# Probabilities times values in matmuls 256 columns wide, and the outputs of attention taken from PSUM by head pair

## The chip, the cores and the metric

The kernel runs on one core of a Trainium2 chip. Its time is the device time in microseconds, the median of three runs. The engines of the core are called PE (TensorE matmuls), PEld (its weight loads), DVE (VectorE), ACT (ScalarE), POOL (GpSimd) and SP (SyncE, which here only issues DMAs). Each engine works through its instructions in order; engines wait for each other by semaphores.

## The reference

One encoder layer over 512 tokens of width 1024, in float32. Two attentions run on one projection of the normalised input, their outputs are normalised, projected and added, and a mixture of experts follows.

```python
qa, ka, va, cq, ckv, kr = jnp.split(h @ w_in[l], IN_SPLITS, axis=-1)
out_a = windowed_gqa_sink(qa, ka, va, a_sink[l])     # A: 8 heads in 2 groups, |i-j| <= 128, a sink logit per head
out_b = mla_attention(q_nope, q_rope, k_nope, k_rope, v_b)   # B: 8 heads, all 512 keys
mixed = jnp.concatenate([rms_norm(out_a, out_norm_a_g[l]), rms_norm(out_b, out_norm_b_g[l])], axis=-1) @ w_out[l]
h = layer_norm(DEEPNORM_ALPHA * h + mixed, ln_attn_g[l], ln_attn_b[l])
ffn = hierarchical_moe(h, ...)    # top group of 4, top 2 of its 8 experts; 32 experts of 1024 -> 2 x 256 -> 1024
h = layer_norm(DEEPNORM_ALPHA * h + ffn, ln_ffn_g[l], ln_ffn_b[l])
```

Inside both attentions a head's output is `softmax(scores) @ v`, with 64 columns of v per head.

## The kernel before

Tokens are cut into four query tiles of 128 (t = 0 to 3). The stages are: layer norm and input projection (up to about 110 us), the two low-rank projections of B (to about 152), attention B (to about 240), attention A (to about 310), a hand-ordered tail that finishes tile 3, routes the tokens and gathers the first rows (to about 345), and the experts in 16 pairs with a closing layer norm. Up to the tail the order on each engine is set by a scheduler that lists instructions by priority and by a modelled time; in A the attention's own instructions are raised in priority by 200 (`tc.high_priority(200)`). The tail and the experts stand in an order written out by hand.

A unit of attention is one tile and one head. `attend` (L601) walks over 32 units, tile by tile and head by head. In step i it makes the scores of unit i, the transposes of unit i-2, and, every second step, the value matmuls of units i-4 and i-3. For B the scores are three matmuls of 512 columns into one of two PSUM banks (`scores_b`, L563, by `mm3`, L212); DVE takes the row maximum (L568), ACT the exponential with its row sum (L571), DVE the reciprocal (L557), and DVE or POOL, by the parity of the head, multiplies by it (L558). `probs_t` (L593) turns the 128x512 probabilities with four PE transposes (L596) and copies them to SBUF (L598), ACT and DVE in turn in B, ACT alone in A. The value matmuls (L619) hold 64 columns of v as weights and stream 128 columns of turned probabilities; head h0 of a pair goes to output partitions 0 to 63, head h1 to 64 to 127, each accumulated over the key tiles (4 in B, 2 or 3 in A). A tile's eight heads fill one PSUM bank (`pac`, of which there is one) in four 128-column parts.

When a tile is done, `finish` (L528) copies the bank to SBUF as a high part (`oh`, ACT) and a low part (`ol`, DVE), squares it (ACT), adds the squares of the four parts (DVE, L537), and projects: 2 x 4 triples of matmuls of 512 columns (L213 to L215 into `pwo`), one summing matmul (L547) for the norm, and an addition to the residual z (L552). `finish` is a generator: `tick` moves it on by a part after each unit, one generator at a time in B and two in A, so that projections fill PE between units. Tile 3 of A is finished in the tail (L1028 to L1085) instead.

The weights of an expert are gu (2 MB, gate and up) and dn (1 MB, down), in a ring of six slots in SBUF; the slots' space is lent to attention first (`tag=`). SP issues their loads in program order, and a load waits at the head of the queue until its space is free. In step 12 of A the kernel asks for pair 0 (slots 0 and 1, gu and dn), and gu of slots 3 and 4 (L1006 to L1008); after the tail for gu2 and dn2 (in the space of A's queries and keys), gu5, dn5, dn4, dn3 (L1226 to L1229), and then for each next pair as a slot comes free.

Of the kernel before, what the change touches and what calls it, by code (L numbers as in the profile page):

```python
# [26 lines left out]
H = 8  # L27
# [44 lines left out]
def build(tc, A, out):  # L72
# [24 lines left out]
    with top:  # L97
# [430 lines left out]
        def finish(t, po, wo):  # L528

            woh, wol = wo  # L530
            oh = fin.tile([P, 4, P], F32R, name="aoh", bufs=2)
            ol = fin.tile([P, 4, P], F32R, name="aol", bufs=2)
            split(po.rearrange("p (a b) -> p a b", a=4), oh, ol)
            sq = fin.tile([P, 4, P], F32, name="asq")
            SC.activation(sq.rearrange("p a b -> p (a b)"), po, AF.Square)
            s1 = fin.tile([P, P], F32, name="asum")
            V.tensor_reduce(s1, sq.rearrange("p a b -> p b a"), AX.X, ALU.add)  # L537
            yield
            for c in range(2):
# [14 lines left out]

        def normed(pr, den, n, eng):
# [7 lines left out]
        def scores_b(t, h):  # L563
# [8 lines left out]
            return normed(pr, den, S, V if h % 2 else PO)  # L572

        def scores_a(t, h):
# [16 lines left out]
            return normed(pr, den, nk, V)  # L591

        def probs_t(pr, n, ev):  # L593
# [3 lines left out]
            pT = scr.tile([P, S], F32, name="pT", bufs=3)  # L597
            ev(pT[:, :n * P], pt[:, :n * P])  # L598
            return pT

        def attend(units, done, hook, width, evs, boost=ExitStack):  # L601

            prs, pts = {}, {}
            n = len(units)
            for i in range(n + 3):
                with boost():
                    if i < n:
                        t, h, sfn = units[i][:3]
                        prs[i] = sfn(t, h)
                    if 2 <= i < n + 2:  # L610
                        pts[i - 2] = probs_t(prs.pop(i - 2), units[i - 2][5], evs[i % 2])
                    if i >= 4 and i % 2 == 0:
                        (t, h0, _, vfn, k0, nk), h1 = units[i - 4], units[i - 3][1]
                        if h0 == 0:
                            po = pac()
                        pp = pts.pop(i - 4), pts.pop(i - 3)
                        for k in range(nk):
                            for j, h in enumerate((h0, h1)):
                                PE.matmul(po[64 * j:64 * j + 64, h0 // 2 * P:h0 // 2 * P + P], vfn(k0 + k, h),  # L619
                                          pp[j][:, k * P:(k + 1) * P], start=(k == 0), stop=(k == nk - 1))  # L620
                        if h1 == H - 1:
                            done(t, po)
# [3 lines left out]
        wob = wout(woh, wol, 512, gob, lambda k: bp.tile([P, D], F32, name="wfo", bufs=2))  # L626
# [5 lines left out]
        attend([(t, h, scores_b, lambda k, h: vb[k][:, h, :], 0, NT) for t in range(NT) for h in range(H)],  # L632
               lambda t, po: side.append(finish(t, po, (woh, wol))), later, 1, (SC.copy, V.tensor_copy))
# [364 lines left out]
        units = []  # L998
        for t in range(NT):
            k0, k1 = max(0, t - 1), min(NT, t + 2)  # L1000
            units += [(t, h, scores_a, lambda k, h: va[:, k, 64 * (h // 4):64 * (h // 4) + 64], k0, k1 - k0)
                      for h in range(H)]
# [542 lines left out]
```

## Time and profile before

| | us |
|---|---|
| median of 3 runs | 599.52 (599.49 to 602.42) |
| profiled execution | 598.21 |
| its span, first to last instruction | 596.6 |
| PE busy in the span | 533.2 (89%) |
| DVE, ACT, POOL busy | 332.9, 204.5, 124.5 |
| moved by DMA | 141.8 MB, 238 GB/s on average |

The profile is of one execution. A busy PE is not a PE at its peak, since the printed duration of a matmul reaches to its modelled end and overlaps the next; what one costs in a stream is read from start to start. Times within the trace count from the span's start.

### The profile page before, as it was taken

To read this page: it belongs to the slowest core of one execution; us is meant where nothing else is said; L and a number is where in the kernel's file an instruction comes from. 1 tells how busy PE (TensorE), PEld (TensorE's weight loads), DVE (VectorE), ACT (ScalarE), POOL (GpSimd) and SP (SyncE) were. 2 spreads that over 40 slices of the span, in tenths; PEclk is the share of its full clock that TensorE was granted. 3 is DMA by queue.
4 is the path that set the end of the run, shared out by engine and by line. 5 is a ranking of instruction groups with operands and counts; after the bars stand their busy time and mean duration, and the time that the engine had idled before them with its cause. 6 is when DMAs were issued, how large, how long until landed. Compare 5 with 4: busy or idle time off the path is not lost. (4 is left out here: it accounts for less than half of the span.)

```text
span 596.6 us, 8402 instructions
## 1 busy us (share of the span) xinstructions
PE 533.2 (89%) x2946; PEld 343.5 (58%) x2947; DVE 332.9 (56%) x887; ACT 204.5 (34%) x429; POOL 124.5 (21%) x157
## 2 busy tenths in 40 slices
PE   2899999999899999999998989999998699879860
PEld 1688898799777777777777643443443233323230
DVE  5946473765777765988867744435334222102277
ACT  2266442454564453766441221211111111102132
POOL 2701121311433332213100121122211101100041
PEclk9999999999899999999998999999999989979985
DMA  8973400421211003992034899999999999999663
GB/s 286 299 256 77 132 11 1 129 81 41 88 37 37 1 1 107 331 421 105 36 142 182 306 345 414 418 414 417 417 413 397 421 419 405 406 424 415 261 271 141
DMA packets 46268, 141.77 MB, mean 238 GB/s; under 512 B 12379, under 2 KB 19419, under 8 KB 37008
## 3 DMA queue, kind: packets, MB, share of 16 engines
q1 hardware_dynamic: 40608, 131.06, 57.6%
q0 software_dynamic: 4464, 8.06, 3.6%
q10 hardware_dynamic: 1152, 2.10, 0.9%
q8 instruction: 24, 0.39, 0.3%
q14 instruction: 20, 0.16, 0.1%
HBM read 133.14 MB, written 16.25 MB: 250 GB/s over the span
## 5 line engine op out<-in xcount | busy, mean ns | idle before, releaser
L1184 PE MATMUL p_gu<-w_gu,xT 128*64 128x512 f32 x512 | 125.7, 614 | 15.2 <-DMA w_gu<-in_w_gu 14.3
L1184 PEld LDWEIGHTS p_gu<-w_gu,xT 128*64 128x64 f32 x512 | 40.7, 141 | 95.4 <-issue 68.0
L1189 DVE TENSOR_TENSOR hid<-hid,p_gu 128x256 f32<-128x256 f32 x16 | 6.7, 421 | 113.0 <-ACT hid L1188 113.0
L1188 ACT ACTIVATE hid<-p_gu 128x256 f32<-128x256 f32 x16 | 6.1, 384 | 176.8 <-PE p_gu L1184 165.0
L1204 PE MATMUL p_y<-w_dn,hidT 128*64 128x512 f32 x256 | 58.5, 598 | 1.0 <-issue 0.6
L1217 DVE SCALAR_TENSOR_TENSOR xg<-p_y,wsl,xg 128x512 f32<-128x512 f32 x30 | 23.5, 790 | 25.8 <-PE p_y L1204 25.3
L995 POOL DMA_INDIRECT xg<-norm_rows,tok x16 | 16.5, 1030 | 101.5 <-issue 23.7
L1210 POOL DMA_INDIRECT moe_rows<-xg,idx x15 | 15.6, 1038 | 98.9 <-DVE xg L1217 74.2
L596 PE MATMUL ptr<-cst,pr 128*128 128x128 f32 x208 | 35.3, 282 | 0.0
L1204 PEld LDWEIGHTS p_y<-w_dn,hidT 128*64 128x64 f32 x256 | 17.1, 136 | 30.3 <-issue 28.2
L558 POOL TENSOR_SCALAR pr<-pr,rc 128x512 f32<-128x512 f32 x16 | 25.0, 1564 | 44.1 <-DVE rc L557 44.1
L598 ACT COPY pT<-ptr 128x512 f32<-128x512 f32 (+2 forms) x48 | 22.6, 477 | 30.4 <-PE ptr L596 26.3
L596 PEld LDWEIGHTS ptr<-cst,pr 128*128 128x128 f32 x208 | 24.8, 143 | 7.7 <-issue 4.7
L571 ACT ACTIVATE pr<-pmm,bnm 128x512 f32<-128x512 f32 x32 | 22.0, 689 | 16.1 <-DVE bnm L568 13.5
L568 DVE TENSOR_REDUCE bnm<-pmm 128x1 f32<-128x512 f32 x32 | 21.8, 685 | 4.6 <-PE pmm L215 4.4
L215 PE MATMUL pmm<-wh,htl 128*128 128x512 f32 (+1 forms) x64 | 23.9, 374 | 0.0
L213 PE MATMUL pmm<-wh,hth 128*128 128x512 f32 (+1 forms) x64 | 23.8, 372 | 0.0
L619 PE MATMUL pac<-pT,vb 128*64 128x128 f32 x256 | 23.7, 282 | 0.0
L214 PE MATMUL pmm<-wl,hth 128*128 128x512 f32 (+1 forms) x64 | 23.5, 368 | 0.0
L590 ACT ACTIVATE pr<-sm,anm 128x257 f32<-128x257 f32 (+1 forms) x32 | 18.1, 567 | 10.2 <-PE ptr L596 5.9
L558 DVE TENSOR_SCALAR pr<-pr,rc 128x512 f32<-128x512 f32 (+2 forms) x48 | 20.9, 440 | 1.1 <-PE pmm L581 0.5
L215 PE MATMUL pwo<-wh,htl 128*128 128x512 f32 (+1 forms) x56 | 20.7, 370 | 0.0
(334 smaller groups left out, 1178.3 us busy)
## 6 DMA issues: line engine op xcount, KB each, us to landing
w_gu<-in_w_gu SPq DMA_DIRECT2D x52, 1024.0 KB, 16.6
w_dn<-in_w_dn SPq DMA_DIRECT2D x20, 1024.0 KB, 18.5
w_dn<-in_w_dn SPq DMA_DIRECT2D x24, 512.0 KB, 14.6
w_gu<-in_w_gu SPq DMA_DIRECT2D x24, 512.0 KB, 16.6
wf<-in_w_in SPq DMA_DIRECT2D x12, 512.0 KB, 6.5
moe_rows<-zr SPq DMA_DIRECT2D x8, 512.0 KB, 7.0
rows<-moe_rows SPq DMA_DIRECT2D x8, 512.0 KB, 8.8
wf<-in_w_q_b SPq DMA_DIRECT2D x12, 192.0 KB, 2.4
```

The lines of the kernel that those rows point to most:

```text
L213: PE.matmul(ps, ah, bh, start=first, stop=False)
L214: PE.matmul(ps, ah, bl, start=False, stop=False)
L215: PE.matmul(ps, al, bh, start=False, stop=last)
L558: eng.tensor_scalar(pr[:, :n], pr[:, :n], rc, None, ALU.mult)
L568: V.tensor_reduce(nm, sp, AX.X, ALU.max, negate=True)
L571: exps_.append(SC.activation(pr[:, :S], sp, AF.Exp, bias=nm, accum_out=den).ins)
L596: PE.transpose(pt[:, k * P:(k + 1) * P], pr[:, k * P:(k + 1) * P], ident)
L598: ev(pT[:, :n * P], pt[:, :n * P])
L619: PE.matmul(po[64 * j:64 * j + 64, h0 // 2 * P:h0 // 2 * P + P], vfn(k0 + k, h), pp[j][:, k * P:(k + 1) * P], start=(k == 0), stop=(k == n ...
L1184: PE.matmul(pg[64 * i:64 * i + 64], xT[:, j, 64 * i:64 * i + 64], ws[i][0][j], start=(j == 0), stop=(j == 7))
L1204: r = PE.matmul(py[64 * i:64 * i + 64, :], hT[:, j, 64 * i:64 * i + 64], ws[i][1][n][:, j], start=(j == 0), stop=(j == 1))
L1217: V.scalar_tensor_tensor(y, py, pl["wsl"], y, ALU.mult, ALU.add)
```

## The change

The value matmuls get 256 columns: in B a unit is still one tile and one head, but two tiles go together (`tp`), and for a pair of heads (`hp`) the four units' turned probabilities stand side by side by tile, so that one matmul streams both tiles of a head. In A two heads of a group, which have the same values, stand side by side; the two groups go to the two halves of the output partitions. That puts A's heads in another order on the partitions, and the rows of w_out and its gain are put in that order on the host.

In B, the bank `pac` is now filled per pair of heads and of tiles (128 x 256) and emptied each time: two casts and a square on ACT, two subtractions and an addition of squares on DVE (`out_b`). `finish` is left for A, its projection is `project` for both; the reduction of squares on DVE is gone, and A's squares are summed by four matmuls instead of one. The multiplication by the reciprocal goes from POOL and DVE to ACT and DVE, half and half (in A: from DVE alone). The space of dn0 serves to stage B's half of w_out and to hold the outputs of tiles 2 and 3, that of dn1 holds turned probabilities of A; so the loads of dn0 and dn1 leave the early group and follow dn2.

```diff
+        def project(t, oh, ol, sums, wo):
...
-                            PE.matmul(sp[:, 0:1], s1, iota1[:, 0:1], start=True, stop=True)
+                            for q, s1 in enumerate(sums):
+                                PE.matmul(sp[:, 0:1], s1, iota1[:, 0:1], start=(q == 0), stop=(q == len(sums) - 1))
...
-            eng.tensor_scalar(pr[:, :n], pr[:, :n], rc, None, ALU.mult)
+            if eng is SC:
+                SC.mul(pr[:, :n], pr[:, :n], rc)
+            else:
+                eng.tensor_scalar(pr[:, :n], pr[:, :n], rc, None, ALU.mult)
...
-            return normed(pr, den, S, V if h % 2 else PO)
+            return normed(pr, den, S, SC if t % 2 else V)
...
-            return normed(pr, den, nk, V)
+            return normed(pr, den, nk, SC if h // 4 else V)
...
+        def out_b(tp, hp, pT):
+            po = pac()
+            for k in range(NT):
+                for j in range(2):
+                    PE.matmul(po[64 * j:64 * j + 64, :2 * P], vb[k][:, 2 * hp + j, :],
+                              pT[j][:, k].rearrange("p a b -> p (a b)"), start=(k == 0), stop=(k == NT - 1))
...
+            for i in range(2):
+                split(pv[:, i], ohs[i][:, hp], ols[i][:, hp])
+            if hp == 0:
+                SC.activation(s1, pv, AF.Square)
+            else:
+                sq = tpb.tile([P, 2, P], F32, name="bsq", bufs=2)
+                SC.activation(sq, pv, AF.Square)
+                V.tensor_tensor(s1, s1, sq, ALU.add)
+            if hp == 3:
+                for i in range(2):
+                    side.append(project(2 * tp + i, [ohs[i][:, k] for k in range(4)], [ols[i][:, k] for k in range(4)],
+                                        [s1[:, i]], (woh, wol)))
...
+        def out_a(t, quad, pT, k0, nk):
...
+            for k in range(nk):
+                for g in range(2):
+                    PE.matmul(po[64 * g:64 * g + 64, 2 * P * quad:2 * P * quad + 2 * P], va[:, k0 + k, 64 * g:64 * g + 64],
+                              pT[g][:, k].rearrange("p a b -> p (a b)"), start=(k == 0), stop=(k == nk - 1))
...
-                h2["w0"] = load_pair(0, (0, 1))
+                h2["w0"] = [load_gus(i, i) for i in range(2)]
...
         gu2, dn2 = load_gus(2, 2), load_dn(2, 2)
+        h2["w0"] = [(gu, load_dn(i, i)) for i, gu in enumerate(h2["w0"])]
```

How it moves instructions is seen in the listing of each engine's program. On PE, at the first head pairs of B, before (L596 the transposes, L619 the value matmuls of a pair of heads, L213 to L215 the scores):

```order
L596 MATMUL ptr<-cst,pr 128x128 x4
L619 MATMUL pac<-pT,vb_1174 64x128
L213 MATMUL pmm<-kth,qth 128x512
L214 MATMUL pmm<-ktl,qth 128x512
L215 MATMUL pmm<-kth,qtl 128x512
L596 MATMUL ptr<-cst,pr 128x128 x4
L619 MATMUL pac<-pT,vb_1174 64x128
L619 MATMUL pac<-pT,vb_1175 64x128 x2
L619 MATMUL pac<-pT,vb_1176 64x128 x2
L619 MATMUL pac<-pT,vb_1177 64x128 x2
```

The same place now (L604 the transposes, L638 the value matmuls of two heads and two tiles):

```order
L604 MATMUL ptr<-cst,pr 128x128 x8
L213 MATMUL pmm<-kth,qth 128x512
L214 MATMUL pmm<-ktl,qth 128x512
L215 MATMUL pmm<-kth,qtl 128x512
L638 MATMUL pac<-pTb,vb_1174 64x256
L213 MATMUL pmm<-kth,qth 128x512
L214 MATMUL pmm<-ktl,qth 128x512
L215 MATMUL pmm<-kth,qtl 128x512
L604 MATMUL ptr<-cst,pr 128x128 x8
```

In both, a group of value matmuls is split: the first one stands alone and the other seven stand together further on. Such a group comes once per two units before and once per four now. Over all of B the listing of before has 31 uninterrupted runs of value matmuls, of 128 in all, and that of now 13, of 64.

On PE in the middle of A, tile 1, before (L580 and L581 the scores, L547 a tile's sum):

```order
L580 MATMUL pmm<-kall,q_85 128x384
L581 MATMUL pmm<-kall,q_85 128x384
L619 MATMUL pac<-pT,va 64x128 x2
L596 MATMUL ptr<-cst,pr 128x128
L619 MATMUL pac<-pT,va 64x128
L596 MATMUL ptr<-cst,pr 128x128
L619 MATMUL pac<-pT,va 64x128
L596 MATMUL ptr<-cst,pr 128x128
L619 MATMUL pac<-pT,va 64x128
L596 MATMUL ptr<-cst,pr 128x128 x3
```

A group of A now (L586 and L587 the scores, L1046 the value matmuls, `pTa` the turned probabilities of one group of heads):

```order
L1046 MATMUL pac<-pTa_2936,va 64x256
L586 MATMUL pmm<-kall,q_85 128x384
L587 MATMUL pmm<-kall,q_85 128x384
L1046 MATMUL pac<-pTa_2969,va 64x256
L1046 MATMUL pac<-pTa_2936,va 64x256
L1046 MATMUL pac<-pTa_2969,va 64x256
L1046 MATMUL pac<-pTa_2936,va 64x256
L1046 MATMUL pac<-pTa_2969,va 64x256
L604 MATMUL ptr<-cst,pr 128x128 x6
```

A's runs become fewer and longer: 32 with 80 matmuls before, 15 with 40 now.

On SP, the loads between the last of the early group and gu5 (`w_gu_3832` and `w_gu_3834` are gu2, `w_dn_3836` is dn2, `w_dn_3838` to `w_dn_3843` are dn0 and dn1, `w_gu_3846` is gu5), now:

```order
L692 DMA w_gu_2896<-in_w_gu 128x2048
L692 DMA w_gu_3832<-in_w_gu 128x2048
L692 DMA w_gu_3834<-in_w_gu 128x2048
L712 DMA w_dn_3836<-in_w_dn 128x2048
L709 DMA w_dn_3838<-in_w_dn 128x1024
L709 DMA w_dn_3839<-in_w_dn 128x1024
L709 DMA w_dn_3842<-in_w_dn 128x1024
L709 DMA w_dn_3843<-in_w_dn 128x1024
L692 DMA w_gu_3846<-in_w_gu 128x2048
```

Before, dn0 stood right behind the mask and dn1 among the early gu loads, and gu5 followed dn2 directly.

## Rows read from the trace of the kernel before

**Rows 1.** The page's slices: the span in 40 equal parts, the mean share of the DMA engines in tenths.

```profile
DMA  8973400421211003992034899999999999999663
```

**Rows 2.** Busy time by engine in a stretch of the experts' stage; the columns are the length in us, then for each engine its busy time and its instructions, then the clock granted to PE as a share of full speed, the mean DMA share and GB/s.

```profile
350.00:560.00 210.00, 190.06 (x902) 75.12 (x902) 67.00 (x178) 31.75 (x45) 29.60 (x28) 0.98 1.01 410
```

**Rows 3.** The same view in slices of 5 us around the end of attention A.

```profile
305.00:310.00 5.00, 5.00 (x45) 3.98 (x45) 2.87 (x17) 1.37 (x4) 0.55 (x1) 1.00 0.09 39
310.00:315.00 5.00, 4.64 (x31) 3.69 (x29) 2.52 (x6) 1.81 (x4) 0.55 (x1) 1.00 0.00 0
315.00:320.00 5.00, 5.00 (x29) 3.86 (x29) 3.53 (x12) 0.00 (x0) 0.00 (x0) 1.00 0.01 3
```

**Rows 4.** The timeline of SP's DMA issues there, gu2's second half and gu5: start, time, line, target and source, count; merged issues stand under their first.

```profile
298.68 0.33 SPq L653 DMA_DIRECT2D w_gu<-in_w_gu  x1
...
319.74 0.80 SPq L653 DMA_DIRECT2D w_gu<-in_w_gu  x2
```

**Rows 5.** Busy time by engine in the stretch of B, in that of A, and in one slice of 5 us of B (columns as in rows 2).

```profile
152.60:240.20 87.60, 85.46 (x586) 64.58 (x584) 62.99 (x142) 45.46 (x105) 29.52 (x28) 0.98 0.16 53
240.20:310.00 69.80, 68.68 (x454) 52.36 (x454) 58.68 (x196) 40.87 (x110) 14.64 (x38) 1.00 0.56 213
...
175.00:180.00 5.00, 4.62 (x31) 3.17 (x30) 4.55 (x11) 4.57 (x9) 1.56 (x1) 1.00 0.53 134
```

**Rows 6.** Groups of instructions of PE in both attentions: busy time and mean ns of one, then the engine's idle time before them and what ended it.

```profile
L619 PE MATMUL pac<-pT,va 128*64 128x128 f32 x160 | 18.7, 288 | 0.8 <-ACT pT L598 0.8
L213 PE MATMUL pmm<-kth,qth 96*128 96x512 f32 x32 | 15.3, 478 | 1.7 <-ACT pr L571 1.7
```

**Rows 7.** The timeline of PE in B, at the end of A's scores, and in the tail: start, time to the modelled end of the last of a merged row, line, target and sources, count.

```profile
166.08 0.43 PE L619 MATMUL pac<-pT,vb 128*64 128x128 f32 x2
166.44 0.50 PE L213 MATMUL pmm<-kth,qth 96*128 96x512 f32 x1
166.78 0.39 PE L214 MATMUL pmm<-ktl,qth 96*128 96x512 f32 x1
...
167.93 0.40 PE L214 MATMUL pmm<-ktl,qth 96*128 96x512 f32 x1
168.16 0.40 PE L215 MATMUL pmm<-kth,qtl 96*128 96x512 f32 x1
168.49 1.09 PE L619 MATMUL pac<-pT,vb 128*64 128x128 f32 x14
169.50 0.66 PE L596 MATMUL ptr<-cst,pr 128*128 128x128 f32 x4
170.09 0.43 PE L619 MATMUL pac<-pT,vb 128*64 128x128 f32 x2
...
173.21 0.66 PE L619 MATMUL pac<-pT,vb 128*64 128x128 f32 x8
173.80 1.10 PE L596 MATMUL ptr<-cst,pr 128*128 128x128 f32 x8
...
298.37 0.28 PE L581 MATMUL pmm<-kall,q 128*128 128x256 f32 x1
...
311.87 1.05 PE L1085 MATMUL psd<-cst,asq 128*128 128x1 f32 x8 [0.26 <-ACT asq L1076]
312.78 0.48 PE L1028 MATMUL pwo<-woah,aoh 128*128 128x512 f32 x1
```

**Rows 8.** The timeline of PE in the experts' stage: the down projection of a pair, eight matmuls of 512 columns that go to the two halves of the columns in turn, and what starts after it.

```profile
425.88 3.65 PE L1204 MATMUL p_y<-w_dn,hidT 128*64 128x512 f32 x16
429.36 4.03 PE L1184 MATMUL p_gu<-w_gu,xT 128*64 128x512 f32 x18
```

**Rows 9.** Groups of ACT and of POOL (columns as in rows 6): in B, in A, and, the last two, over the span.

```profile
L558 POOL TENSOR_SCALAR pr<-pr,rc 128x512 f32<-128x512 f32 x16 | 25.0, 1564 | 44.1 <-DVE rc L557 44.1
L571 ACT ACTIVATE pr<-pmm,bnm 128x512 f32<-128x512 f32 x32 | 22.0, 689 | 16.1 <-DVE bnm L568 13.5 <-DVE rc L557 1.4 <-PE ptr L596 1.1
L598 ACT COPY pT<-ptr 128x512 f32<-128x512 f32 x16 | 9.3, 584 | 18.9 <-PE ptr L596 18.8
L571 ACT ACTIVATION_READ_ACCUMULATOR pr<-pmm,bnm 128x1 f32 x32 | 6.3, 197 | 0.0
L535 ACT ACTIVATE asq<-pac 128x512 f32<-128x512 f32 x3 | 1.8, 594 | 0.5 <-DVE aol L209 0.5
...
L590 ACT ACTIVATE pr<-sm,anm 128x385 f32<-128x385 f32 x16 | 9.9, 619 | 7.9 <-PE ptr L596 5.9 <-issue 1.3 <-DVE rsq_t L181 0.4
L774 ACT ACTIVATE z<-z,ln_nb,ln_rs 128x512 f32<-128x512 f32 x2 | 1.5, 804 | 0.0
...
L420 ACT COPY va<-pmm 128x128 f32<-128x128 f32 x2 | 0.5, 272 | 0.4 <-DVE rp L329 0.4
L410 ACT ACTIVATE junk<-pmm 128x256 bf16<-128x256 f32 x4 | 1.5, 379 | 1.8 <-PE pmm L215 1.8
```

**Rows 10.** Groups of DVE, in B and in A.

```profile
L537 DVE TENSOR_REDUCE asum<-asq 128x128 f32<-128x512 f32 x3 | 3.2, 1061 | 0.0
L209 DVE TENSOR_TENSOR aol<-pac,aoh 128x512 fp32r<-128x512 f32 x3 | 2.1, 684 | 0.9 <-ACT aoh L208 0.9
...
L558 DVE TENSOR_SCALAR pr<-pr,rc 128x384 f32<-128x384 f32 x16 | 7.1, 454 | 0.1
```

**Rows 11.** ACT's preparation of B's half of w_out: its group in B (columns as in rows 6).

```profile
L524 ACT ACTIVATE wobh<-wfo,gob 128x1024 fp32r<-128x1024 f32 x4 | 4.6, 1149 | 0.9 <-DMA wfo<-in_w_out 0.9
```

More of the change, by code (lines that the diff above doesn't have):

```diff
@@ L553, in finish @@
                 yield
+        def finish(t, po, wo):
+            oh = fin.tile([P, 4, P], F32R, name="aoh", bufs=2)
+            ol = fin.tile([P, 4, P], F32R, name="aol", bufs=2)
+            split(po.rearrange("p (a b) -> p a b", a=4), oh, ol)
+            sq = fin.tile([P, 4, P], F32, name="asq")
+            SC.activation(sq.rearrange("p a b -> p (a b)"), po, AF.Square)
+            yield
+            yield from project(t, [oh[:, k] for k in range(4)], [ol[:, k] for k in range(4)], [sq[:, k] for k in range(4)], wo)
         def normed(pr, den, n, eng):
@@ L596, in probs_t, with attend @@
                 PE.transpose(pt[:, k * P:(k + 1) * P], pr[:, k * P:(k + 1) * P], ident)
[L597 to L603, printed above, removed]
+            ev(dest, pt[:, :n * P].rearrange("p (a b) -> p a b", a=n))
+        def attend(units, hook, width, evs, boost=ExitStack):
+            prs = {}
             n = len(units)
@@ L607, in attend @@
                     if i < n:
-                        t, h, sfn = units[i][:3]
-                        prs[i] = sfn(t, h)
+                        prs[i] = units[i][0]()
                     if 2 <= i < n + 2:
[L611 to L622, printed above, removed]
+                        probs_t(prs.pop(i - 2), units[i - 2][1](), evs[i % 2])
+                    if i >= 3 and units[i - 3][2]:
+                        units[i - 3][2]()
                 tick(width)
                 hook(i)
-        wob = wout(woh, wol, 512, gob, lambda k: bp.tile([P, D], F32, name="wfo", bufs=2))
+        wob = wout(woh, wol, 512, gob, lambda k: m3.tile([P, D], F32, name="wfo", tag=f"dn0{k % 2}"))
         def later(i):
@@ new lines, in units_b, with dest @@
+        def units_b(tp, hp):
+            pT = {}
+            def dest(j, i):
+                if i == 0:
+                    pT[j] = tpb.tile([P, NT, 2, P], F32, name="pTb", bufs=3)
+                return pT[j][:, :, i]
+            return [(lambda t=2 * tp + i, h=2 * hp + j: scores_b(t, h), lambda j=j, i=i: dest(j, i),
+                     (lambda: out_b(tp, hp, pT)) if i and j else None) for j in range(2) for i in range(2)]
+        attend([u for tp in range(2) for hp in range(4) for u in units_b(tp, hp)], later, 1, (SC.copy, V.tensor_copy))
@@ L634, in build @@
+        tbs.close()
         bst.close()
@@ L1530 @@
     for name in _INS:
-        give(name, inputs[name])
+        if name not in ("w_out", "out_norm_a_g"):
+            give(name, inputs[name])
     gate, up = [np.asarray(inputs[n])[0].reshape(NE, NK, P, FF) for n in ("w_gate", "w_up")]
@@ L1536 @@
     give("w_dn", np.asarray(inputs["w_down"])[0].reshape(NE, 2, P, 2, 512).transpose(0, 2, 3, 1, 4).reshape(NE, P, 4, 512))
+    w_out = np.asarray(inputs["w_out"])
+    heads = w_out[:, :512].reshape(1, 2, 4, 64, D).transpose(0, 2, 1, 3, 4).reshape(1, 512, D)
+    give("w_out", np.concatenate([heads, w_out[:, 512:]], axis=1))
+    give("out_norm_a_g", np.asarray(inputs["out_norm_a_g"]).reshape(1, 2, 4, 64).transpose(0, 2, 1, 3).reshape(1, 512))
     c = shape_constants()
```

51 lines of the change are left out of this document (32 added, 19 removed).

## The prediction

> **What bounds the kernel now.** I read the page's slices first, then the stretches around the loads, the SP queue, the two attention stretches, and last the PE timeline inside them. From about 350 us on the DMA engines are full: share 1.01 at 410 GB/s over 210 us, while PE works for 190 of them [rows 1, 2]. That is the stream of expert weights; its end moves only with its start. Before it, between 305 and 320 us, the DMA engines move almost nothing (shares 0.09, 0.00, 0.01) although weights are still to come [rows 3]: the SP queue issued gu2's second half at 298.7, and dn2 right behind it, when the last scores released their space, and gu5 only at 319.7, when the attention's tail had released its own [rows 4]. So the start of the stream hangs on the end of attention, and there is slack of some 15 us of DMA time ahead of it.
>
> Attention itself is PE's. In B's stretch (152.6 to 240.2) PE is busy 85.5 of 87.6 us, in A's (240.2 to 310) 68.7 of 69.8; DVE has 63.0 and 58.7, ACT 45.5 and 40.9 [rows 5]. What PE waited for in both is small: 1.7 us before a score matmul and 0.8 before the value matmuls are the largest entries [rows 6]. A microsecond taken from PE there is therefore a microsecond off the end, as long as PE stays the bound: I take the transfer to the end as one to one.
>
> **What a 128-column value matmul costs.** Each value matmul is two instructions of the trace, for two halves of the array's columns in turn. I call an uninterrupted run of them a segment and read it from start to start, since the printed durations overlap [rows 7]. One matmul (x2): 166.08 to 166.44, 0.36 us. Seven (x14): 168.49 to 169.50, 1.01. The difference over six more is 0.109 each, which is the spacing of the plain transposes too, and 0.145 stays over per segment: an odd number n takes n+1 such slots (the first and last instruction have no partner), an even one n slots (x8: 173.21 to 173.80, 0.59 = 4 x 0.109 + 0.155). Around a segment more is lost. The score matmul before it takes 0.33 to the next start (168.16 to 168.49) where its twin takes 0.23: 0.10 on entry. After it the first score takes 0.34 (166.44 to 166.78), again 0.10 more, and four transposes between two segments take 0.59 (169.50 to 170.09) for 0.44 + 0.10 + 0.05. I use 0.175 for entry and exit together. A segment costs 0.32 us besides its slots.
>
> At 512 columns a slot costs 0.43: x16, eight matmuls, from 425.88 to 429.36 [rows 8]. That is four times 0.109. So the time of a slot goes with its columns, and 256 columns cost 0.2145. The wider matmuls save nothing by their width; the change saves by unpaired slots and by fewer segments.
>
> The Trainium skill says otherwise: "TensorE: Matmul & The Clock Gate", section "Back-to-back issue gap", gives a sustained spacing of about 81 ns at 128 columns and 131 ns at 512, so far less than in proportion. By it a column at 256 would cost some 40% less than at 128, and the 27.0 us of slots below would be about 16 (an estimate from that page). This trace disagrees (0.109 against 0.43), and I go by the trace.
>
> **The sum on PE.** Counted in the listing of PE's order, of which front rows show pieces: before, B has 128 value matmuls in 31 segments (28 of odd length), 156 slots; A has 80 in 32 (28 odd), 108 slots. That is 264 x 0.109 = 28.8, plus 63 x 0.147 = 9.3, plus 63 x 0.175 = 11.0: 49.1 us. After, B has 64 in 13 segments, 74 slots; A 40 in 15, 52 slots: 126 x 0.2145 = 27.0, plus 28 x 0.147 = 4.1, plus 28 x 0.175 = 4.9: 36.0 us. Saved: 13.1, of which 35 vanished segments make 35 x 0.32 = 11.3 and the unpaired slots the rest.
>
> Added on PE: without the summing reduction on DVE, each A tile's squares need four column sums instead of one. Eight such instructions take 0.91 us (311.87 to 312.78) [rows 7], so 3 tiles x 6 x 0.114 = 2.1 us. Tile 3 had four already, B keeps one. Net: 11.0 us less on PE.
>
> **The other engines.** POOL loses 16 multiplications of 1.56 us, ACT gets them: the shape SBUF to SBUF with one factor per partition is not in the trace at 512 columns, so I bound it by a copy (0.584) and by an ACTIVATE with two such operands (0.804), and take the exp's 0.689, which has one. That is 16 x 0.69 = 11.0 in B and, by A's longer exp (0.62) and somewhat less for the tiles with fewer keys, 16 x 0.56 = 9.0 in A [rows 9]. The exits from PSUM by head pair: eight times two casts of 128x128 (0.272) and one square of 128x256 (0.38), 7.4, for four times 0.58 + 0.59 = 4.7. ACT goes from 86.3 to 86.3 + 11.0 + 9.0 + 2.7 = 109 of some 146 us. DVE loses seven reductions of 1.06 and A's sixteen multiplications (0.45, fewer keys less), 14 us, and gets about 7 of small pieces (16 subtractions near 0.3, 6 additions near 0.4, an estimate from 0.68 at 512 columns) for 2.7 [rows 10]: 122 becomes 112. On average PE is still the bound, so these cost nothing by themselves.
>
> Not so early in B. The projections, which fill PE while a unit's chain runs, need two tiles now; ahead of unit 24 the listing has 4 of their triples of matmuls, where before it had 12. B's values are by the sum above 74 x 0.2145 + 13 x 0.32 = 20.1 us, 0.63 per unit. Up to unit 24 PE has 24 x (scores 0.705 + transposes 0.436 + values 0.63) + 2.8 = 45.3 us. ACT has per unit exp 0.886 with its accumulator read, half a multiplication 0.345, half a copy 0.292 and a quarter of an exit 0.23: 24 x 1.75 + four weight preparations of 1.15 = 46.6. Two engines with equal work, each in order, do not both run full. The stall is at least 1.3 us (ACT never idle); at most, if ACT fills no more than its fullest slice of before (4.57 of 5 us at 175 to 180) [rows 5], 46.6/0.914 - 45.3 = 5.7. I take 4, nearer the upper end, because DVE, with 4.55 of 5 us in that same slice, has no room either. Later PE has the projections' backlog and is the bound again; work delayed there is not lost. In A the values wait on nothing new: each of its four tiles of turned probabilities has its own space.
>
> **Loads.** The four 512 KB halves of pair 0's dn weights leave the early group and stand behind dn2 on SP, 2.1 MB or 5.1 us at 410 GB/s. dn0's space is free once B's last projections are done, dn1's after A's last value matmul. Both are then issued inside the 15 us of empty DMA and land before gu5 is due, all of it shifted alike. I cost them at nothing; without that cover they cost 5.1. The w_out halves move behind the mask on SP; their use on ACT waited 0.9 us for a load in all, and PE needs the result only with the projections: nothing [rows 11]. The reordering of w_out is on the host.
>
> **Result.** 11.0 - 4 = 7 us off. The profiled execution took 598.2 us (span 596.6 and 1.6 around it), so 591.2; the median of the runs is 1.3 above it, so 592.5.
>
> **Rivals.**
> 1. ACT sets the pace through all of B. For it: the equal sums above, and its queue order has exps, multiplications, casts and weight preparation in one line. Against it: over all of B ACT has 45.5 + 11.0 + 2.7 = 59 us of some 80, and PE has a backlog from unit 24 on. If the stall is 9 us instead of 4: 597.5. The Trainium skill has the matching warning, "TensorEngine Tiling (Array Packing)", section "PSUM Bottleneck": tiling speeds up TensorE but not the emptying of PSUM, which one should do in large pieces; this trace shows the price of small ones, 0.272 for a quarter of 0.584.
> 2. Slower: one PSUM bank for all of B's value outputs. Before, it was emptied once per tile; now eight times, by two casts and a square on ACT and two subtractions on DVE, behind exps in their queues. PE is in order, so a value matmul that finds the bank full stops scores and transposes too. Units are about 2 us apart and the next group comes four units later, so some 6 us are there for some 2 us of work; it decides from a wait of 0.9 us per group (8 x 0.9 = 7). At 2.3 us per group: 8 x 2.3 = 18 against 7, 603.5.
> 3. The dn loads are not covered (dn1 late, or gu5 held behind it): +5.1, 597.6. Against it: the empty slices.
> 4. Width does count, as the page has it: 11 us more saved, 581.5. Against it: the 512-column row.
> 5. It doesn't do what it says: the segments stay. The order listing excludes that.
>
> **Chances.** Forecast 0.60 (own range 588.5 to 596), rival 1 0.18, rival 2 0.10, rival 3 0.07, rival 4 0.05. About 0.5% (3 us) is what a measurement here can tell from no change. Faster by more: 0.60 + 0.05 + 0.05 of rivals 1 and 3 = 0.70; slower by more: nearly all of rival 2, 0.09; within: 0.21. The range for 8 in 10 runs from 587.5, where nothing stalls and entries cost a bit more, to 599.5, which takes in rivals 1 and 3.
>
> **What would show it.** Value matmuls at 0.215 per slot and 28 segments in all; the last scores some 6 to 8 us earlier than 298.4 [rows 7]; idle on PE of a few microseconds named after ACT before about 200 us and hardly any after; dn1 landed before gu5 is issued; gu5 issued near 312.7; the stream at 410 GB/s as before. It is wrong if PE waits for the bank's emptying at each group, if the DMA engines have no empty slices left before gu5, or if a slot at 256 columns is well under 0.21.

## The result, and the profile after

The changed kernel takes 592.75 us in the median of six runs (591.04 to 594.98), the kernel before 600.10 in six beside them: a ratio of 0.9875, 95% interval 0.9844 to 0.9907. The forecast was 592.5. The profiled execution has a span of 589.5 us, 7.1 under that of before.

The page's slices of the DMA engines answer to [rows 1], and the stretches to [rows 2, 3, 5] (columns as there). The last two stretches are slices of B.

```profile
DMA  8983310221201005991266799999999999999663
```

```profile
152.60:240.20 87.60, 83.19 (x485) 60.22 (x484) 66.11 (x176) 63.07 (x159) 5.07 (x17) 0.98 0.23 73
240.20:310.00 69.80, 68.62 (x407) 52.75 (x405) 49.49 (x163) 42.53 (x109) 14.87 (x34) 1.00 0.55 203
305.00:310.00 5.00, 4.71 (x33) 4.10 (x32) 2.70 (x6) 0.32 (x1) 0.55 (x1) 1.00 0.41 149
310.00:315.00 5.00, 3.90 (x23) 2.84 (x22) 4.38 (x17) 0.59 (x1) 0.00 (x0) 1.00 0.16 26
...
350.00:560.00 210.00, 188.53 (x888) 72.37 (x886) 63.32 (x171) 30.52 (x44) 28.63 (x27) 0.98 0.99 402
...
175.00:180.00 5.00, 4.49 (x27) 3.14 (x23) 4.20 (x9) 3.32 (x7) 0.00 (x0) 1.00 0.60 206
180.00:185.00 5.00, 3.42 (x17) 2.03 (x17) 4.98 (x10) 5.00 (x14) 0.00 (x0) 1.00 0.02 6
```

The stream from 350 us on is as before (0.99 for 1.01). Its start moved. SP's issues, after, for [rows 4] (the first row merges the four loads of dn0 and dn1, the second the two of gu5):

```profile
292.88 10.80 SPq L709 DMA_DIRECT2D w_dn<-in_w_dn  x4
313.26 0.81 SPq L692 DMA_DIRECT2D w_gu<-in_w_gu  x2
```

gu5 is issued at 313.26 for 319.74. From there to the end of the span it is 276.2 us, before 276.9. So nearly all of the gain is won ahead of gu5, and it reaches the end one to one.

To compare executions I count from B's first score matmul, since its own time differs by up to 2.4 us between the executions below. The first row is of the kernel before, the others of the changed one, for [rows 7]:

```profile
152.60 0.48 PE L213 MATMUL pmm<-kth,qth 96*128 96x512 f32 x1
```

```profile
153.37 0.48 PE L213 MATMUL pmm<-kth,qth 96*128 96x512 f32 x1
...
163.96 0.65 PE L638 MATMUL pac<-pTb,vb 128*64 128x256 f32 x2
164.54 0.50 PE L213 MATMUL pmm<-kth,qth 96*128 96x512 f32 x1
...
167.01 1.94 PE L638 MATMUL pac<-pTb,vb 128*64 128x256 f32 x14
168.88 0.50 PE L213 MATMUL pmm<-kth,qth 96*128 96x512 f32 x1
...
291.71 0.28 PE L587 MATMUL pmm<-kall,q 128*128 128x256 f32 x1
```

From the first scores to gu5's issue it was 319.74 - 152.60 = 167.14 us and is 313.26 - 153.37 = 159.89: 7.25 us less. Below, a run of value matmuls is what the prediction calls a segment, and a slot is as there. One matmul of 256 columns (x2, two slots) takes 0.58 us to the next start, seven (x14, eight slots) take 1.87: six more cost 1.29, which is 0.215 each, and 0.15 is left over per run.

Summing every matmul of that stretch, from its start to the next one's start less any gap between them, tells where the 7.25 come from (us; B's scores are in "all else", 26.82 and 26.95):

| | before | after | difference |
|---|---|---|---|
| value matmuls | 37.98 | 31.62 | -6.4 |
| transposes | 26.36 | 22.39 | -4.0 |
| A's scores | 12.43 | 11.88 | -0.6 |
| column sums | 2.42 | 4.09 | +1.7 |
| all else | 84.33 | 84.31 | 0.0 |
| gaps, PE idle | 3.62 | 5.60 | +2.0 |

The gaps grew in the first 45 us of B only (2.14 to 4.18). The profile's list of waits of PE from 150 to 245 us names ACT for all of it:

```profile
PE pmm L213 <- ACT pr L577: 2.6, 2, 1.7
PE ptr L604 <- ACT pr L562: 1.4, 2, 1.2
PE pwo L213 <- ACT wobh L524: 0.4, 1, 0.4
```

(The longest, 1.7, is the start of B and stands before too.) The groups that the change priced, in B and, the last two, in A (columns as in [rows 6]; for [rows 9, 10]):

```profile
L562 ACT ACTIVATE pr<-pr,rc 128x512 f32<-128x512 f32 x16 | 11.6, 725 | 0.8 <-DVE rc L560 0.7
...
L655 ACT ACTIVATE bsq<-pac 128x256 f32<-128x256 f32 x6 | 2.3, 380 | 0.5 <-DVE aol L209 0.5
...
L208 ACT CAST aoh<-pac 128x128 fp32r<-128x128 f32 x8 | 2.1, 263 | 0.5 <-PE pac L638 0.3
...
L209 DVE TENSOR_TENSOR aol<-pac,aoh 128x128 fp32r<-128x128 f32 x8 | 2.3, 282 | 0.5 <-ACT aoh L208 0.5
...
L562 ACT ACTIVATE pr<-pr,rc 128x384 f32<-128x384 f32 x8 | 5.0, 622 | 2.9 <-DVE rc L560 2.8
...
L562 ACT ACTIVATE pr<-pr,rc 128x256 f32<-128x256 f32 x5 | 2.5, 507 | 0.0
```

### The profile page after: what moved, and what is told of

It reads as the page before. It is cut to its first block, busy times and chain, and to the rows that moved or that the text cites. A ratio compares the mean times of both kernels' runs of the same rounds, so it can differ in the third digit from the quotient of the medians.

```text
span 589.5 us, 8004 instructions
## 1 busy us (share of the span) xinstructions
PE 523.4 (89%) x2756; PEld 331.8 (56%) x2757; DVE 322.6 (55%) x882; ACT 222.1 (38%) x477; POOL 99.9 (17%) x141
## 5 line engine op out<-in xcount | busy, mean ns | idle before, releaser
L1263 PE MATMUL p_y<-w_dn,hidT 128*64 128x512 f32 x256 | 59.9, 611 | 1.0 <-issue 0.6
L604 PE MATMUL ptr<-cst,pr 128*128 128x128 f32 x208 | 33.3, 278 | 1.9 <-ACT pr L562 1.4
L1269 POOL DMA_INDIRECT moe_rows<-xg,idx x15 | 15.6, 1039 | 95.0 <-DVE xg L1276 69.6
L604 PEld LDWEIGHTS ptr<-cst,pr 128*128 128x128 f32 x208 | 24.9, 145 | 9.5 <-ACT pr L562 3.2
L215 PE MATMUL pmm<-wh,htl 128*128 128x512 f32 (+1 forms) x64 | 24.0, 374 | 0.0
L213 PE MATMUL pmm<-wh,hth 128*128 128x512 f32 (+1 forms) x64 | 23.8, 372 | 0.0
L214 PE MATMUL pmm<-wl,hth 128*128 128x512 f32 (+1 forms) x64 | 23.5, 368 | 0.0
L562 ACT ACTIVATE pr<-pr,rc 128x512 f32<-128x512 f32 (+2 forms) x32 | 20.6, 645 | 4.1 <-DVE rc L560 3.9
L590 DVE CUSTOM_DVE_ANT_0 sm<-pmm,mask,nsink 128x256 f32<-128x256 f32 (+1 forms) x32 | 17.4, 545 | 7.6 <-PE pmm L587 6.5
L215 PE MATMUL pwo<-wh,htl 128*128 128x512 f32 (+1 forms) x56 | 20.7, 370 | 0.0
L214 PE MATMUL pwo<-wl,hth 128*128 128x512 f32 (+1 forms) x56 | 20.5, 367 | 0.0
L213 PE MATMUL pwo<-wh,hth 128*128 128x512 f32 (+1 forms) x56 | 20.5, 367 | 0.0
L1232 ACT ACTIVATE xg<-xg,of 128x1024 f32<-128x1024 f32 x15 | 17.2, 1149 | 8.5 <-PE p_x L1228 7.8
```

The lines of the kernel that those rows point to most:

```text
L213: PE.matmul(ps, ah, bh, start=first, stop=False)
L214: PE.matmul(ps, ah, bl, start=False, stop=False)
L215: PE.matmul(ps, al, bh, start=False, stop=last)
L562: SC.mul(pr[:, :n], pr[:, :n], rc)
L590: V.tensor_tensor_reduce(sm[:, :nk], sp[:, :nk], mask[:, mo:mo + nk], 1.0, nsink[:, h:h + 1], ALU.add, ALU.min, nm)
L604: PE.transpose(pt[:, k * P:(k + 1) * P], pr[:, k * P:(k + 1) * P], ident)
```

## The experiments

All twelve, in one table. "Between" is the time from B's first scores to gu5's issue in the profiled execution, "idle" the sum of PE's gaps in the first 45 us of it. Ratios are to the kernel before on the same chip, with 95% intervals; e9 and e10 were timed once each. "Between" and "idle" are of one execution each: e7 leaves attention as it was, and differs from before by 0.6 and 0.4 us, so less than that says nothing.

| | first scores | gu5 issued | between | idle | time, us | ratio |
|---|---|---|---|---|---|---|
| before | 152.60 | 319.74 | 167.14 | 2.14 | 600.10 | |
| changed kernel | 153.37 | 313.26 | 159.89 | 4.18 | 592.75 | 0.9875 (0.9844 to 0.9907) |
| e1 narrow | 154.12 | 317.04 | 162.92 | 4.54 | 596.87 | 0.9955 (0.9928 to 0.9981) |
| e2 one piece | 152.01 | 309.38 | 157.37 | 4.08 | 589.09 | 0.9825 (0.9792 to 0.9859) |
| e3 POOL multiplies | 152.26 | 313.45 | 161.19 | 3.77 | 591.94 | 0.9890 (0.9840 to 0.9940) |
| e4 reduction back | 152.80 | 310.23 | 157.43 | 3.97 | 590.88 | 0.9871 (0.9820 to 0.9921) |
| e5 B alone | 152.87 | 313.94 | 161.07 | 4.17 | 594.18 | 0.9908 (0.9880 to 0.9936) |
| e6 A alone | 153.96 | 320.07 | 166.11 | 2.56 | 600.10 | 0.9992 (0.9976 to 1.0008) |
| e7 late dn | 154.16 | 320.73 | 166.57 | 2.57 | 601.62 | 1.0010 (0.9988 to 1.0032) |
| e8 ACT multiplies | 152.29 | 312.75 | 160.46 | 3.91 | 592.67 | 0.9868 (0.9846 to 0.9890) |
| e9 late projections | 151.72 | 319.89 | 168.18 | 2.36 | 597.34 | |
| e10 spread preparation | 152.42 | 310.96 | 158.54 | 2.93 | 589.32 | |
| e11 two banks | 153.17 | 303.19 | 150.02 | 3.55 | 582.90 | 0.9719 (0.9694 to 0.9744) |
| e12 e11 with one bank | 153.70 | 308.19 | 154.49 | 4.28 | 587.43 | 0.9782 (0.9731 to 0.9833) |

**e1: the width taken back, the grouping kept.**

```diff
-            for k in range(NT):
-                for j in range(2):
-                    PE.matmul(po[64 * j:64 * j + 64, :2 * P], vb[k][:, 2 * hp + j, :], pT[j][:, k]..., ...)
+            for i in range(2):
+                for k in range(NT):
+                    for j in range(2):
+                        PE.matmul(po[64 * j:64 * j + 64, P * i:P * i + P], vb[k][:, 2 * hp + j, :], pT[j][:, k, i], ...)
...
```

> The changed kernel with each value matmul of 256 columns cut into two of 128 (B tile by tile, A head by head), all else the same. The listing has 41 runs of value matmuls (238 slots) for 28 (126 slots). Theory (a slot's time goes with its columns; the change gains by fewer runs and fewer unpaired slots): 238 x 0.109 = 25.9 us of slots for 27.0, and 13 runs more at 0.28 = +3.6: gu5 issued 2 to 4 us later than in the changed kernel (315 to 317), time about 595. Rival (width counts: 256 columns cost little more than 128): a slot at 256 would be about 0.13, so halving the width costs some 10 us: gu5 near 323, 603.

Between grew by 3.0 us, within the theory's 2 to 4; the rival wanted 10. The value matmuls themselves took 31.98 us for 31.62, though twice as many and half as wide: by slots 238 x 0.109 + 41 x 0.147 = 32.0. Most of what was lost lies in the transposes (+1.3) and A's scores (+0.8), between which the 13 additional runs stand. Columns cost what they cost at either width. Against before, whose values took 37.98, nearly all that the values gained is kept at 128 columns: it came from the grouping. The width did count in another way: of the 35 runs fewer (63 to 28), 22 are gone in e1's listing, and the other 13 go only with the width.

**e2: groups in one piece.**

```diff
-                for j in range(2):
+                for j in (1, 0):
...
-                for g in range(2):
+                for g in (1, 0):
```

> The changed kernel with the two heads of a value group in the other order, so that the first matmul of a group needs the probabilities that are turned last; a group then stands in one piece. The listing has 20 runs with 108 slots for 28 with 126. Theory (PE is the bound, unpaired slots and runs are what values cost besides their columns): 18 x 0.2145 + 8 x 0.28 = 6.1 us off PE: last scores near 286, gu5 issued near 307.2, 586.5. Rival A (the early single matmuls filled time in which PE would stand idle): the idle time of PE before the transposes and scores grows by as much, gu5 within 1.5 us of 313.3. Rival B (a group that stands together holds up the scores behind it, ACT and DVE run dry): later than 313.3.

The values fell by 5.3 us, as the slots say (108 x 0.2145 + 20 x 0.147 = 26.1, measured 26.31). Between fell by 2.5 only. Gaps of PE took 1.2 of the rest, and a wait appeared that the changed kernel does not have: a group's first matmul for the emptying of the one bank. In the waits, and in the timelines of PE and ACT:

```profile
PE pac L638 <- ACT bsq L655: 1.0, 1, 1.0
```

```profile
183.51 0.60 PE L604 MATMUL ptr<-cst,pr 128*128 128x128 f32 x4
185.07 1.95 PE L638 MATMUL pac<-pTb,vb 128*64 128x256 f32 x16 [0.96 <-ACT bsq L655]
```

```profile
184.15 0.59 ACT L605 COPY pTb<-ptr 128x512 f32<-128x512 f32 x1 [1.52 <-PE ptr L604]
184.63 0.39 ACT L655 ACTIVATE bsq<-pac 128x256 f32<-128x256 f32 x1
```

The square that frees the bank stood in ACT's queue behind a copy that itself waited for PE's transposes. The remaining 1.6 us went to other groups (transposes +0.5, A's scores +0.6, projections and the rest); what lengthened these was not followed up. Theory right in kind, at less than half of its price.

**e3: B's sixteen multiplications of ACT on POOL.**

```diff
-            return normed(pr, den, S, SC if t % 2 else V)
+            return normed(pr, den, S, PO if t % 2 else V)
```

> The changed kernel with B's 16 multiplications of ACT (11 us) given to POOL. The listing has 30 runs of value matmuls with 126 slots for 28 with 126, so +0.5 us of work on PE. Theory (in B's first 24 units ACT has as much work as PE and stalls it by about 2 us): idle of PE in 170 to 190 goes from 2.5 us to under 1, last scores about 1.5 us earlier, 590 to 591.5. Rival A (ACT paces all of B): 5 us or more earlier, 587. Rival B (POOL's 1.56 us a multiplication makes the chain of a unit longer, and PE waits for it): later by 1 us or more, 594 and up, with waits of PE named after POOL.

Neither as expected: idle fell by 0.4 us only, and between grew by 1.3. The transposes took 24.15 us for 22.39, which more than makes up for that and is not explained. Of the gaps, those of 172 to 184 us fell from 2.5 to 0.7 us, but 1.3 us of new ones came at 160 to 168, where a multiplication of POOL takes 1.6 us:

```profile
163.38 1.70 POOL L564 TENSOR_SCALAR pr<-pr,rc 128x512 f32<-128x512 f32 x1 [1.99 <-DVE rc L560]
165.87 1.57 POOL L564 TENSOR_SCALAR pr<-pr,rc 128x512 f32<-128x512 f32 x1 [0.79 <-DVE rc L560]
```

That POOL's time is what those gaps waited for was not tested further; the time stayed within the measurement's bounds.

**e4: the summing reduction back on DVE, one column sum in A's tiles.**

```diff
+            s1 = fin.tile([P, P], F32, name="asum")
+            V.tensor_reduce(s1, sq.rearrange("p a b -> p b a"), AX.X, ALU.add)
             yield
-            yield from project(t, ..., [sq[:, k] for k in range(4)], wo)
+            yield from project(t, ..., [s1], wo)
```

> The changed kernel with A's summing reduction given back to DVE (1.06 us a tile), one summing matmul instead of four for the tiles 0 to 2 of A. Theory (PE is the bound in A): 18 summing matmuls fewer, 1.7 to 2.0 us, and 2 slots of value matmuls more (+0.4): gu5 issued 1.2 to 1.6 us earlier, near 312, 591.3. Rival (A is no longer bound by PE, or DVE's 3 us come into the path): no gain or up to 3 us later.

Between fell by 2.5 us: 1.85 of column sums (4.09 to 2.24), 0.75 of gaps, and 0.3 lost in the values. So the column sums cost PE 1.85 us, and what the dropped reduction took off DVE did not pay for them. The interval of the time, on four runs, still takes in the changed kernel's.

**e5 and e6: the two halves alone.** B alone (A's units as before, in the changed loop), and A alone (B's units as before). A piece of e5's edit; e6 does the like to B's units.

```diff
-            return [(lambda h=4 * g + 2 * quad + j: scores_a(t, h), ..., (lambda: out_a(t, quad, pT, ...)) if g and j else None) ...]
+            return [(lambda h=h: scores_a(t, h), lambda h=h: dest(h), (lambda h=h: out_a(t, h, pts, ...)) if h % 2 else None) for h in range(H)]
...
```

> The change in B alone: A's value matmuls, its multiplications, its summing reduction and the order of w_out's rows as in the kernel before; the dn loads late as in the changed kernel. The listing has 13 runs of B's value matmuls with 74 slots (before 31 with 156) and, since A starts otherwise, 27 runs of A's with 100 slots (before 32 with 108). Theory: values 3.8 us less in B and 1.6 in A, entries and exits 23 x 0.13 = 3.0 less, 2.0 more of idle time on PE before 200 us: gu5 6.4 us earlier than before's 319.7, near 313.3, time 593. Rival (most of the gain was A's): gu5 after 317, time 597 or more.

> The change in A alone: B's value matmuls, their exit from PSUM, the multiplications on POOL and DVE and the reduction as in the kernel before; the dn loads late and w_out's staging as in the changed kernel. The listing has 18 runs of A's value matmuls with 52 slots, before 32 with 108. Theory: values 2.7 us less, entries and exits 14 x 0.13 = 1.8 less, sums 1.7 more, no added idle time in B: gu5 2.8 us earlier than 319.7, near 316.9, time 597. Rival (the gain was A's): gu5 near 313, time 593.

B alone took 6.1 us off between, A alone 1.0: together 7.1 of the 7.25. B was as expected (6.4) and is nearly all of the gain. A fell short of its 2.8; its 1.0 is little more than the 0.6 by which e7 differs, and its time shows no change. Its value matmuls should take 52 x 0.2145 + 18 x 0.147 = 13.8 us and took 15.6, with hardly a gap between them in PE's rows; three runs are 0.4 to 0.7 us longer than their slots. The waits of the weight loads, from 240 to 310 us, have it:

```profile
PEld pac L1033 <- ACT pTa L610: 2.2, 6, 0.5
```

A run starts before its second head's turned probabilities are copied, and waits in its middle. Such a wait shows on PEld alone.

**e7: the kernel before, with dn0 and dn1 behind dn2.**

```diff
-                h2["w0"] = load_pair(0, (0, 1))
+                h2["w0"] = [load_gus(i, i) for i in range(2)]
...
         gu2, dn2 = load_gus(2, 2), load_dn(2, 2)
+        h2["w0"] = [(gu, load_dn(i, i)) for i, gu in enumerate(h2["w0"])]
```

> The kernel before with its dn0 and dn1 loads moved behind dn2, nothing else. Theory (15 us of DMA time stand empty ahead of gu5, 5.1 us of loads fit): gu5 issued at 319.7 as before, ratio 1.000 within 0.3%. Rival (the loads are not covered): up to 5.1 us later, ratio 1.008.

A ratio of 1.001, within its interval no change, and between 166.57 for 167.14. The loads are covered; 5.1 us, or 1.008, is outside of the interval.

**e8: all of B's multiplications on ACT.**

```diff
-            return normed(pr, den, S, SC if t % 2 else V)
+            return normed(pr, den, S, SC)
```

> The changed kernel with all of B's multiplications on ACT (16 more, 11 us). The listing has 11 runs of B's value matmuls with 68 slots for 13 with 74, 1.8 us less on PE. Theory of the prediction (in the first 24 units ACT's work is what PE waits for; 46.6 us grows by 12 x 0.69 = 8.3): idle of PE before 205 us grows from 4.2 to 10 or more, gu5 at 318 or later, time 597 or more. Rival, which the run with POOL speaks for (the stall is the chain of a unit with nothing to fill it, not the amount of work on ACT): idle grows by less than 2, gu5 at 311 to 314, 590 to 593.

The prediction's step falls. ACT has some 11 us more to do in B, and PE's idle did not grow (3.91 for 4.18). It was not free, though: the value matmuls took 1.7 us less, and between is still 0.6 longer; the transposes took 1.4 more. Here PE and ACT do have equal work. The stretch from B's first scores to those of the 24th unit, up to which the prediction counted, in the changed kernel and in e8 (PE, PEld, DVE, ACT, POOL):

```profile
153.37:200.50 47.13, 42.95 (x249) 30.46 (x246) 39.23 (x91) 37.66 (x87) 1.35 (x4) 0.96 0.16 50
```

```profile
152.29:199.46 47.17, 43.26 (x245) 29.80 (x242) 34.00 (x79) 43.01 (x97) 1.35 (x4) 0.96 0.17 50
```

With equal work, 43.3 and 43.0 us, both fit into 47.2, and 1.7 of PE's 3.9 us of gaps is the start of B. e8's next stretches show that an engine on the path of every unit can be filled further than the 0.914 on which I set the stall:

```profile
170.00:180.00 10.00, 9.20 (x54) 5.95 (x53) 7.77 (x16) 9.74 (x19) 0.00 (x0) 1.00 0.28 75
180.00:190.00 10.00, 9.15 (x55) 6.19 (x54) 8.18 (x18) 9.95 (x24) 0.00 (x0) 1.00 0.08 32
```

**e9: the kernel before without projections to fill PE early in B.** After e8 I held that PE lacked work to fill a unit's chain.

```diff
-                tick(width)
+                if i >= hold:
+                    tick(width)
...
-            if i >= 8:
+            if i >= 18:
...
+            g = finish(t, po, (woh, wol))
+            next(g)
+            side.append(g)
...
+               begun, later, 1, (SC.copy, V.tensor_copy), hold=24)
```

> The kernel before with B's projections held back: the weights of w_out are prepared from step 18 on for step 8, and the projections of tiles 0 and 1 follow from step 24 on (a tile still leaves PSUM at once). Ahead of the 21st unit's scores the listing has none of the triples of projection matmuls that before has there (8), ahead of the 25th 6 for 16. Theory now (the added idle time of the changed kernel is PE with nothing to fill a unit's chain, since its projections need two tiles): the idle time of PE in the first 45 us after B's first scores grows from 2.1 us by 1.5 to 5.6 (the 8 triples take 5.6), though ACT and POOL have no instruction more. Rival (it comes from the changed kernel's small exits and its groups of four units): it grows by less than 0.5.

This theory falls too: with no projection ahead of the 21st unit, idle grew by 0.2 us. The edit holds back the preparations of w_out as well (the first on ACT at 190.75 us, before at 170.93), so it shows that missing projections alone leave no gaps, and not what they do together with the preparations.

**e10: the preparation of w_out spread.** A look at ACT's timeline in the changed kernel gave the third theory:

```profile
175.96 0.76 ACT L562 ACTIVATE pr<-pr,rc 128x512 f32<-128x512 f32 x1
176.58 0.29 ACT L208 CAST aoh<-pac 128x128 fp32r<-128x128 f32 x1
178.55 1.15 ACT L524 ACTIVATE wobh<-wfo,gob 128x1024 fp32r<-128x1024 f32 x1 [1.68 <-DMA wfo<-in_w_out]
179.60 0.67 ACT L577 ACTIVATE pr<-pmm,bnm 128x512 f32<-128x512 f32 x1
```

```profile
180.42 0.50 PE L213 MATMUL pmm<-kth,qth 96*128 96x512 f32 x1 [0.92 <-ACT pr L577]
...
183.39 1.09 PE L604 MATMUL ptr<-cst,pr 128*128 128x128 f32 x8 [1.17 <-ACT pr L562]
```

ACT stands still for 1.68 us at the head of its queue, waiting for the third part of w_out. An exponential and all behind it wait with it, and PE then stands for 0.92 and 1.17 us. PE's waits name the exponential and the multiplication, not the load. There are two staging buffers; the third load can start when DVE has read the first (174.99 on DVE's timeline), and the wait ends 3.6 us later.

```diff
-            if i >= 8:
+            if i >= 2 and i % 3 == 2:
```

> The changed kernel with the four preparations of w_out (1.15 us each on ACT, more on DVE) spread over steps 2, 5, 8 and 11 of B for four steps in a row from 8 on. Rival to the theory of missing filling (the idle time of 172 to 183 us is the burst of these preparations in ACT's queue ahead of exponentials): idle of PE in the first 45 us falls from 4.2 us to 3.2 or less. Theory of missing filling: it moves, but stays within 0.5 of 4.2. The time from B's first scores to gu5's issue follows the idle time, with 0.2 us for 2 slots more and a run more of value matmuls.

ACT's wait for w_out is gone (its group in the changed kernel, and here):

```profile
L524 ACT ACTIVATE wobh<-wfo,gob 128x1024 fp32r<-128x1024 f32 x4 | 4.6, 1160 | 1.7 <-DMA wfo<-in_w_out 1.7
```

```profile
L524 ACT ACTIVATE wobh<-wfo,gob 128x1024 fp32r<-128x1024 f32 x4 | 4.6, 1142 | 0.0
```

Idle fell to 2.93, and between by 1.35: 1.25 of the 2.0 us that the change had added, in one execution. The other 0.8 us are open. The edit takes away two things at once, the wait for the load and the burst of four preparations, and other runs show that the wait by itself is not it. The same group in e3 and in e6:

```profile
L524 ACT ACTIVATE wobh<-wfo,gob 128x1024 fp32r<-128x1024 f32 x4 | 4.6, 1150 | 1.6 <-DMA wfo<-in_w_out 1.6
```

```profile
L524 ACT ACTIVATE wobh<-wfo,gob 128x1024 fp32r<-128x1024 f32 x4 | 4.6, 1148 | 1.0 <-DMA wfo<-in_w_out 1.0
```

In e3 ACT waits as long, but without multiplications in its queue, and PE's gaps there are 0.7 us for 2.5. In e8 ACT does not wait (0.1 us, no load named) but has more multiplications, and the gaps from 171 to 184 us are still 1.6. And e6 has the changed kernel's staging of w_out with B's units as before: ACT waits 1.0 us, at the fourth part and as before (0.9), and PE's gaps in that stretch are 0.4, as before. So the moved staging is not the cause either. In e6 ACT comes to the third preparation 25.0 us after B's first scores, when its load is there; in the changed kernel, with B's instructions on ACT in another order, after 23.5.

**e11 and e12: the gains together.** e2 and e4 in one kernel; e11 with B's outputs in two banks in turn (the second was unused in this stage), e12 with one.

```diff
-            po = pac()
+            po = ps.tile([P, 512], F32, name="psd", tag="psd") if hp % 2 else pac()
...
```

> The changed kernel with three edits: value groups in one piece as in e2, the summing reduction on DVE as in e4, and B's value outputs in two PSUM banks in turn. Measured from B's first scores to gu5's issue, e2 took 2.5 us off the changed kernel and e4 2.5. In e2 PE waited 1.0 us for the bank to be emptied. Theory (all of it is PE's time, and the parts add): 159.9 - 2.5 - 2.5 - 1.0 = 153.9 us, time 586.5 or less, no wait of a value matmul for the emptying. Rival (what e2 and e4 took off was the same slack in A): 156 to 157.5, time 588 to 590.

> e11 without its second PSUM bank, so e2 and e4 together. The listing has 11 runs of A's value matmuls with 44 slots, e11 8 with 40; B's are alike (8 with 64). From B's first scores to gu5's issue e11 took 150.0 us. Theory (the bank is emptied while PE waits, and the wait makes the rest late): e2 and e4 add, 159.9 - 2.5 - 2.5 = 154.9 us, a wait of PE for the emptying of 1 us or more, time near 588. Rival (the second bank gave only its better order in A, 4 slots and 3 runs, 1.7 us): 151 to 152.5 us, no such wait over 0.3 us, time near 584.5.

e12: 154.49 for 154.9 by the sum, and PE waits for the bank as in e2:

```profile
PE pac L640 <- ACT bsq L657: 1.0, 1, 1.0
```

So the two edits add, against the rival. e11 is another 4.5 us shorter, at 150.02 where its theory had 153.9, without any such wait; that beats both kernels: 582.9 us, a ratio of 0.9719 to before. The bank gave more than the wait that it removed: 1.9 us of gaps, and 1.3 us of value matmuls by its better order in A (4 slots and 3 runs fewer; 26.16 to 24.87). The last 1.3 us are not assigned.

## Why the prediction was right, point by point

**What bounds the kernel.** Right. gu5's issue moved by 6.5 us, the end by 7.1; the stretch that the change touches shrank by 7.25.

**The value matmuls.** The price of a slot holds at 256 columns (0.215 predicted and measured), and so do the 28 runs and the 0.147 over. Values were to fall from 38.1 to 31.1 and fell from 37.98 to 31.62. The Trainium skill's "TensorE: Matmul & The Clock Gate", section "Back-to-back issue gap", would have had the width pay; the trace disagrees (0.109, 0.215 and 0.43 us at 128, 256 and 512), and e1 shows the same without any slot being read: half the width, and the values take 0.4 us more.

**Entry and exit, mis-sized.** I took 0.175 us for each of the 35 runs that vanish, 6.1 us. The transposes and A's scores fell by 4.5, 0.13 each. I had taken the middle of 0.20, read beside B's scores, and 0.15, read between transposes [rows 7]; but B's scores did not fall at all (26.82 and 26.95). That this is a price by the run is not shown either: with 13 runs more e1 has 2.1 us more in transposes and A's scores, but with 8 and 12 fewer than the changed kernel e2 has 1.0 more and e11 (22.45 and 11.86) the same. What else these groups hold was not followed up.

**Column sums.** 2.1 predicted, 1.7 measured. That the reduction's removal from DVE is worth nothing was implied by PE as the bound; e4 agrees, since between is shorter with it.

**ACT.** The multiplications cost 0.725, 0.622 and 0.507 us by width, in place of 0.69 and 0.56, the squares 0.380, the casts 0.263: all near. **The step that failed** is the stall of 4 us from "two engines with equal work". It was 2.0, and the work was not equal. Up to the 24th unit's scores PE has 42.95 us and ACT 37.66, for 45.3 and 46.6 in the prediction. I had added ACT's printed durations, and they overlap as PE's do: in the rows of the changed kernel under e10 a multiplication prints 0.76 us and the next instruction starts after 0.62, a preparation prints 1.15 and the next starts after 1.05. ACT stood idle for 9.5 of the 47.1 us. When e8 did make the work equal, the stall did not grow, and missing projections alone made none (e9).

What reached PE is a wait that I costed at nothing, that for w_out. There I had the right row, ACT's 0.9 us [rows 11], and argued that PE needs the result only later. But ACT works in order, and what PE needs at once stood behind the waiting instruction. The wait grew to 1.7 us, and PE stood for 0.92 and 1.17 us; with the preparations spread, 1.25 of the 2.0 are gone (e10). The wait alone does not make these gaps (0.7 of 2.5 us in e3), and a longer queue without it still leaves 1.6 (e8), so what stands in ACT's queue there has a part in it; how much is whose is not shown, and 0.8 us are open.

So 7 us came out as 11.0 - 4, and is 9.25 - 2.0: two errors of about 2 us that cancel. That the forecast was met to 0.3 us is luck.

**Loads.** Nothing, as said: e7, the last of the four dn loads issued by 303.7 us, and slices at 0.41 and 0.16 of DMA share just ahead of gu5.

**The rivals.** ACT as the pace of all B: against it ACT's 9.5 idle us, and e8. The bank's emptying: not in the changed kernel, whose waits have no value matmul in them; in e2 and e12 it appears as soon as groups stand in one piece, once, at 1.0 us, and e11 removes it. It was a real mechanism at a lower price. The Trainium skill's "TensorEngine Tiling (Array Packing)", section "PSUM Bottleneck", warns that tiling speeds up TensorE but not the emptying of PSUM. The trace agrees in e2 and e12, with that 1.0 us; in the changed kernel no value matmul waits for it. Uncovered loads: e7. Width: e1.

## What to carry to other kernels

Price an order of instructions by how often a stream is interrupted, not only by the width of its pieces: here 35 fewer runs make, by their price, 5.1 of the 6.4 us that the value matmuls gained (35 x 0.147), and swapping the order of two heads, so that no matmul is ready early and alone, gave 2.5 us more for two edited lines. Add up an engine's work from start to start, also on ACT; printed durations gave 46.6 us where the trace has 37.7. A wait at the head of an in-order queue is to be priced by all that stands behind it; the profile names the instruction behind, so follow its engine back to the first idle time. And when a bank is emptied by several small instructions, look at what stands ahead of the last of them before changing when it is filled.

## What the runs showed that I had not expected

A run of value matmuls can wait in its middle without a gap on PE: 2.2 us in e6, seen on the weight loads alone. ACT can be busy for 9.74 and 9.95 of 10 us (e8) without more gaps on PE. And a second bank for outputs was worth 4.5 us (e11 against e12), though the waits that named the bank were 1.0 us in all: the scheduler also found a better order with it.
